# Sixteen more tokens gathered instead of computed densely, in a PEER block on one core

## The chip, the cores and the metric

The kernel runs on one core of a Trainium2 chip. The metric is the device time of one execution in microseconds (us). A profiled execution gives a trace of every engine: TensorE (PE, with its weight loads as PEld), VectorE (DVE), ScalarE (ACT), GpSimd (POOL) and SyncE (SP), which here only issues DMAs.

## What is computed

A residual block over 512 tokens of 1024 features. A token mixer (input projection, a recurrent branch and a convolution branch, output projection) comes first, and then the part that this study is about, a product-key expert layer. For each of 512 tokens and 8 heads it picks 16 of 16384 experts, so 128 experts for a token. An expert n has a row of u and a row of v, 1024 numbers each:

```python
def peer(xn, w_q, sub_keys, u_tab, v_tab):
    ...
    q = (t @ w_q).reshape(n_tok, PEER_HEADS, 2, PEER_HALF)
    sc = jnp.einsum("thpk,hpnk->thpn", q, sub_keys).astype(jnp.float32)
    s_top, i_top = lax.top_k(sc, PEER_TOPK)
    ...
    best, pos = lax.top_k(cand.reshape(n_tok, PEER_HEADS, kk), PEER_TOPK)
    ...
    g = jax.nn.softmax(best, axis=-1).astype(xn.dtype)
    ...
        ue = u_tab[ib]
        act = jax.nn.gelu(jnp.einsum("phkd,pd->phk", ue, tb))
        ve = v_tab[ib]
        return jnp.einsum("phk,phkd->pd", gb * act, ve)
```

Everything is float32. The layer's output is added to its input, and a last RMSNorm follows.

## The kernel before

The tokens are four tiles of 128. Tile 0 is the **gathered** tile: each of its tokens sits on one partition, and for each of its 128 expert choices an indirect DMA on POOL (L362) fetches 128 rows of u (tiles `ru`) or of v (`rv`), half a MB each. VectorE multiplies a `ru` with the tokens and sums along the row (L371); a `rv` is scaled and added into `acc0` (L385). That makes 256 gathers with 256 products of about 1.2 us. The order of the gathers is the list `gsched`; `gather_steps(n, left)` issues the next n of them and runs the waiting products until `left` remain open. The row buffers are three (`GR`) and, from the V stage on, five more (`DR`).

The other three tiles, 384 tokens (`TD`), are **dense**: for all 16384 experts the kernel computes gelu(u·x), multiplies it with a gate matrix that is zero except at the chosen experts, and multiplies the result with v. Experts come in 128 tiles of 128.

- An **h tile** is u·x for 128 experts and 384 tokens: 8 slices of the features, each as three matmuls (`mm3`, L147 to L149, tile `ph`), because a float32 number is split into a high and a low part (`hi_u` by ScalarE, L107; `lo_u` by VectorE or POOL, L108 or L745). `h_act` (L402) applies the gelu into `hg`. The first 56 (`SPILL`) are stored to memory and read back later (`hr`).
- The **top-k stage** (about 380 to 583 us) makes q and the scores on TensorE and the top-16s on VectorE, with an h tile in its steps.
- The **gate stage** (583 to 797 us) builds the gate matrix. It works in subs of 8 tokens (`OC`): VectorE makes two one-hot tensors (`oij` L714, `o12` L716, 2048 elements per partition), TensorE multiplies them, 16 matmuls for a sub (L726, L727, tile `pg`), and ScalarE evicts to the gate tile `stg` (L729). A step is two subs and one h tile (`h_step`). Eight steps fill `stg` for one token tile; there are 24 steps, in three blocks. After the first and the second block `stg`, 8 MB, is stored to memory in four DMAs on SP (L775), and 7 extra h tiles (`HB`) cover the store. In one step of three (`GSTEP`) a gather is issued.
- The **V stage** (797 us to the end) runs over the 128 expert tiles. For each it loads the rows of v, splits them (`hi_v` L107, `lo_v` L108), reads back the gates `gt` (of two token tiles; the third stayed in `stg`) and the stored gelus, multiplies them to `wf` (L847, L848), splits that into `wh` (ScalarE, L849) and `wl` (VectorE, L850), and adds to six PSUM accumulators `acc` with 18 matmuls of 512 columns (`v_mm`, L829, L830, L833). In the first 66 of these tiles an h tile is computed as well (`h_tile`). The gathers that are left are spread by weights: 2 for each of the first 66 tiles, `GTAIL` for the next 58, none for the last four. `GLEFT` products may stay open.

What sets the order: a scheduler is pinned off, so that each engine runs its instructions in the order of the program; queues are FIFO. A gather needs a free row buffer, which the product of an earlier gather releases, and its indices, which ScalarE copies (`eix`, L667).

## Time and profile before

| | |
|---|---|
| time, median of 3 runs | 1619.81 us |
| time, lowest and highest | 1617.53, 1622.06 us |
| time of the profiled execution | 1617.53 us |
| its span | 1615.4 us |
| PE busy | 1595.6 us, 99% |
| DVE busy | 1264.4 us, 78% |
| ACT busy | 688.2 us, 43% |
| POOL busy | 510.8 us, 32% |
| moved by DMA | 379.09 MB, mean 235 GB/s |

The span is what the engines' records cover; the time has a little before and behind it. Matmuls overlap, so a busy PE is not PE at its peak, and the shares are means over stages that have different limits: each stage has to be read by itself.

### The profile page before, as it was taken

What the parts mean: (1) busy time and instruction counts of PE and PEld (TensorE: products, weight loads), DVE (VectorE), ACT (ScalarE), POOL (GpSimd) and SP (SyncE); (2) the same over time, 40 slices, a digit from 0 to 9 for tenths busy, and PEclk for the clock granted to TensorE, in tenths of its full rate; (3) what the DMA queues carried; (4) which work ended last, traced back from release to release, by engine and by line L of the source; (5) the groups of instructions that cost most, each with busy time, mean ns of one, the idle gap of its engine ahead of it and who ended that gap; (6) DMA issues with size and microseconds to landing.
All of it is one profiled execution on the core that took longest, in us unless ns stands there. A gap on an engine that the chain in (4) does not pass through costs nothing.

```text
span 1615.4 us, 23573 instructions
## 1 busy us (share of the span) xinstructions
PE 1595.6 (99%) x8402; PEld 1412.5 (87%) x8402; DVE 1264.4 (78%) x2404; ACT 688.2 (43%) x1222; POOL 510.8 (32%) x379
## 2 busy tenths in 40 slices
PE   9999999999999999999999999999999999999997
PEld 8888888888988999999999888989998988887886
DVE  6666666645999997676878888888888789877767
ACT  7444444434333454454533433344333343333334
POOL 0000000004787840000045554545444554223231
PEclk9999999999999999999999999999999999999999
DMA  6222222334333356969499999999999999998884
GB/s 243 95 95 95 95 95 95 91 112 175 107 124 112 126 180 189 304 214 301 153 317 328 344 324 331 342 328 332 340 335 336 323 334 362 340 320 288 305 305 153
DMA packets 158453, 379.09 MB, mean 235 GB/s; under 512 B 14080, under 2 KB 78592, under 8 KB 158208
## 3 DMA queue, kind: packets, MB, share of 16 engines
q1 hardware_dynamic: 112832, 230.25, 41.6%
q0 software_dynamic: 36864, 134.23, 23.5%
q10 hardware_dynamic: 8640, 13.11, 2.3%
q8 instruction: 65, 1.06, 0.3%
q14 instruction: 52, 0.43, 0.1%
HBM read 345.56 MB, written 31.98 MB: 234 GB/s over the span
## 4 chain that ended last, share of the span: by engine, by line
PE 70%; DVE 9%; DMA 8%; issue 7%; POOL 3%; ACT 1%; SPq 1%; DVEq 0%; POOLq 0%; ACTq 0%
PE ph L147 7%; PE ph L149 7%; PE ph L148 7%; PE acc L830 7%; PE acc L833 6%; PE acc L829 6%; PE pin L149 6%; PE pin L147 6%; PE pin L148 6%; DMA ru<-in_u_tab_dram,eix 4%; DMA rv<-in_v_tab_dram,eix 3%; POOL rv L362 2%; PE pq L147 2%; PE pq L149 2%; PE pq L148 2%
## 5 line engine op out<-in xcount | busy, mean ns | idle before, releaser
L147 PE MATMUL ph<-a1h,hi_u 128*128 128x384 f32 x1024 | 346.3, 338 | 0.0
L149 PE MATMUL ph<-a1h,lo_u 128*128 128x384 f32 x1024 | 343.6, 336 | 0.6 <-POOL lo_u L108 0.4
L148 PE MATMUL ph<-a1l,hi_u 128*128 128x384 f32 x1024 | 342.7, 335 | 0.0
L830 PE MATMUL acc<-lo_v,wh 128*128 128x512 f32 x768 | 301.0, 392 | 5.1 <-DVE lo_v L108 5.1
L829 PE MATMUL acc<-hi_v,wh 128*128 128x512 f32 x768 | 299.5, 390 | 0.0
L362 POOL DMA_INDIRECT rv<-in_v_tab_dram,eix x128 | 168.1, 1313 | 265.0 <-ACT eix L667 229.7
L833 PE MATMUL acc<-hi_v,wl 128*128 128x512 f32 x768 | 238.7, 390 | 0.0
L362 POOL DMA_INDIRECT ru<-in_u_tab_dram,eix x120 | 161.0, 1341 | 216.7 <-ACT eix L667 178.3
L385 DVE SCALAR_TENSOR_TENSOR acc<-rv,w,acc 128x1024 f32<-128x1024 f32 x128 | 164.4, 1285 | 75.8 <-DMA rv<-in_v_tab_dram,eix 75.4
L107 ACT ACTIVATE hi_v<-raw_v 128x1024 fp32r<-128x1024 f32 x128 | 135.0, 1055 | 182.8 <-PE ph L148 169.3
L371 DVE SCALAR_TENSOR_TENSOR ru<-ru,t 128x1024 f32<-128x1024 f32 x128 | 155.7, 1222 | 57.0 <-DMA ru<-in_u_tab_dram,eix 56.9
L148 PEld LDWEIGHTS ph<-a1l,hi_u 128*128 128x128 f32 x1024 | 192.3, 188 | 2.6
L147 PEld LDWEIGHTS ph<-a1h,hi_u 128*128 128x128 f32 x1024 | 192.3, 188 | 2.6
L149 PEld LDWEIGHTS ph<-a1h,lo_u 128*128 128x128 f32 x1024 | 192.1, 188 | 1.5 <-POOL lo_u L108 0.8
L849 ACT ACTIVATE wh<-wf 128x384 fp32r<-128x384 f32 x128 | 67.0, 524 | 268.9 <-PE acc L830 193.0
L830 PEld LDWEIGHTS acc<-lo_v,wh 128*128 128x128 f32 x768 | 144.2, 188 | 38.9 <-DVE lo_v L108 10.1
L149 PE MATMUL pin<-a1h,lo_in 128*128 128x512 f32 x448 | 174.4, 389 | 0.3 <-POOL lo_in L108 0.3
L148 PE MATMUL pin<-a1l,hi_in 128*128 128x512 f32 x448 | 174.4, 389 | 0.0
L147 PE MATMUL pin<-a1h,hi_in 128*128 128x512 f32 x448 | 174.3, 389 | 0.0
L833 PEld LDWEIGHTS acc<-hi_v,wl 128*128 128x128 f32 x768 | 144.1, 188 | 30.7
L829 PEld LDWEIGHTS acc<-hi_v,wh 128*128 128x128 f32 x768 | 144.1, 188 | 27.4 <-ACT hi_v L107 0.2
L108 DVE TENSOR_TENSOR lo_v<-raw_v,hi_v 128x1024 fp32r<-128x1024 f32 x128 | 155.9, 1218 | 3.4 <-ACT hi_v L107 3.4
(199 smaller groups left out, 2469.9 us busy)
## 6 DMA issues: line engine op xcount, KB each, us to landing
raw_u<-in_uT_dram SPq DMA_DIRECT2D x128, 512.0 KB, 5.4
raw_v<-in_v_tab_dram SPq DMA_DIRECT2D x128, 512.0 KB, 5.6
raw_in<-in_w_in_dram SPq DMA_DIRECT2D x56, 512.0 KB, 3.3
gd<-stg SPq DMA_DIRECT2D x8, 2048.0 KB, 17.8
gt<-gd SPq DMA_DIRECT2D x128, 128.0 KB, 5.0
hd<-hg ACTq DMA_DIRECT2D x56, 192.0 KB, 3.4
hr<-hd SPq DMA_DIRECT2D x56, 192.0 KB, 5.5
raw_q<-in_w_q_dram SPq DMA_DIRECT2D x16, 512.0 KB, 3.2
```

Source lines behind the costliest of these rows:

```text
L107: act.activation(hi, raw, AF.Copy)
L108: lo_eng.tensor_tensor(lo, raw, hi, op=ALU.subtract)
L147: pe.matmul(pt, wh(k), xh(k), start=start and m == 0, stop=False)
L148: pe.matmul(pt, wh(k), xl(k), start=False, stop=False)
L149: pe.matmul(pt, wl(k), xh(k), start=False, stop=stop and m == n - 1)
L362: ins = pool.indirect_dma_start(out=rows, out_offset=None, in_=tab, in_offset=bass.IndirectOffsetOnAxis(ap=ix, axis=0))
L371: dq.append(lambda: dve.scalar_tensor_tensor(rows, rows, 1.0, t0, op0=ALU.mult, op1=ALU.mult, accum_out=d0[:, n:n + 1]))
L385: dq.append(lambda: dve.scalar_tensor_tensor(acc0, rows, w0[:, n:n + 1], acc0, op0=ALU.mult, op1=ALU.add))
L829: pe.matmul(accs[t][h], wh[:, ts], hi[:, hsl], start=first, stop=False)
L830: pe.matmul(accs[t][h], wh[:, ts], lo[:, hsl], start=False, stop=False)
L833: pe.matmul(accs[t][h], wl[:, ts], hi[:, hsl], start=False, stop=last)
L849: act.activation(wh, wf, AF.Copy)
```

## The change

The last 16 tokens (`TE`) leave the dense part and are gathered too. For them a gather holds 8 partitions to a token: partition 8e + k works on token e, and 16 gathers of u rows and 16 of v rows (`xxu`, `xxv`) cover their 128 experts each. So:

- h tiles, `hg`, `hr` and `hd` have 368 columns (`TDE`) and no longer 384. `wf` keeps 384 columns, the last 16 of them zeroed once in two fixed buffers; its second product has 112 columns.
- There are 46 subs and not 48: the last gate step has no one-hots and no gate matmuls.
- The normalised last token tile is made once more in rows (`tx`, two POOL operations), its 16 tokens go to memory and are read back with each token on 8 partitions (`te`, 16 DMAs on SP). Indices and gates of the 16 tokens go through memory in the same way (`eed`, `egd`, `ee`, `eg`).
- 32 gathers are added: first the 16 `xxu`, and behind the first head's `ru` the weights (`gather_xw`) and the 16 `xxv`, whose products go to `acce`. At V tile 48 (`XADD`) `acce` is split, and four matmuls of 512 columns sum each token's 8 partitions into the accumulators of the last token tile.
- `GSTEP` is now (1,): from the third gate step on a gather in every step, 22 in the stage and not 8.
- `DR` and `GLEFT` go from 5 to 4, `GTAIL` from 0.5 to 0.7.

```diff
+TE = 16
+TDE = TD - TE
...
-GSTEP = (1, 0, 0)
+GSTEP = (1,)
...
-DR = 5
-GTAIL = 0.5
+DR = 4
+GTAIL = 0.7
...
-GLEFT = 5
+GLEFT = 4
 GR = 3
+XADD = 48
...
+        tx = fp.tile([P, D], F32, tag="junk", name="tx", bufs=1)
+        pool.tensor_scalar(tx, xs[NTT - 1], r, None, op0=ALU.mult)
+        pool.tensor_tensor(tx, tx, n2b, op=ALU.mult)
...
+        act.dma_start(txd, tx[P - TE:, :])
...
+    def gather_xu(n):
+        rows = gather(u_tab, n, f"xxu{n}")
+        dq.append(lambda: dve.scalar_tensor_tensor(rows, rows, 1.0, te, op0=ALU.mult, op1=ALU.mult,
+                                                   accum_out=de[:, n:n + 1]))
...
+    def gather_xv(n):
+        rows = gather(v_tab, n, f"xxv{n}")
+
+        def add():
+            if n == 0:
+                acce.append(gp.tile([P, D], F32, tag="te", name="acce", bufs=1))
+                dve.tensor_scalar(acce[0], rows, de[:, 0:1], None, op0=ALU.mult)
+            else:
+                dve.scalar_tensor_tensor(acce[0], rows, de[:, n:n + 1], acce[0], op0=ALU.mult, op1=ALU.add)
...
-        mm3(pt[:, :TD], lambda k: hi[:, k * P:(k + 1) * P], lambda k: lo[:, k * P:(k + 1) * P],
-            lambda k: a1h[:, k, P:], lambda k: a1l[:, k, P:], range(KD))
+        mm3(pt[:, :TDE], lambda k: hi[:, k * P:(k + 1) * P], lambda k: lo[:, k * P:(k + 1) * P],
+            lambda k: a1h[:, k, P:P + TDE], lambda k: a1l[:, k, P:P + TDE], range(KD))
...
+            if s_ == 8:
+                for e in range(TE):
+                    sync.dma_start(te[e * EK:(e + 1) * EK, :], txd[e:e + 1, :].partition_broadcast(EK))
...
-    gsched = []
+    gsched = [(gather_xu, n) for n in range(TE)]
     for h in range(HEADS):
         for n in range(h * TOPK, (h + 1) * TOPK):
             gsched.append((gather_u, n))
+        if h == 0:
+            gsched.append((gather_xw, 0))
+            gsched.extend((gather_xv, n) for n in range(TE))
...
+        act.dma_start(eed, eall[last[1], last[0], :])
+        act.dma_start(egd, gall[last[1], last[0], :])
+        for e_, d_ in ((ee, eed), (eg, egd)):
+            pool.dma_start(e_, d_.rearrange("e (k n) -> (e k) n", n=TE))
...
-        NSUB = NDT * P // OC
+        NSUB = TDE // OC
...
-                gather_steps(GSTEP[(sub // 2) % len(GSTEP)], 2)
+                if sub // 2 == 1:
+                    act.activation(eei, ee, AF.Copy)
+                if sub // 2 > 1:
+                    gather_steps(GSTEP[(sub // 2) % len(GSTEP)], 2)
...
+    wfs = [dp.tile([P, TD], F32, name=f"wf{m}") for m in range(2)]
+    for wf in wfs:
+        dve.memset(wf[:, TDE:], 0.0)
...
-        dve.tensor_tensor(wf[:, TG:], stg[:, i, :], hv_[:, TG:], op=ALU.mult)
+        dve.tensor_tensor(wf[:, TG:TDE], stg[:, i, :P - TE], hv_[:, TG:], op=ALU.mult)
...
+        if i == XADD:
+
+            bf = dp.tile([P, TG], F32, tag="gt", name="bf", bufs=4)
+            br = strm.tile([P, TD], F32R, tag="wh", name="br", bufs=3)
+            dve.memset(bf[:, :P], 0.0)
+            dve.tensor_reduce(bf[:, P - TE:P], ident.rearrange("p (e k) -> p e k", k=EK), op=ALU.add, axis=AX.X)
+            act.activation(br[:, :P], bf[:, :P], AF.Copy, scale=GSC)
+            hi, lo = split(acce[0], "acce", dve)
+            for part in (hi, lo):
+                for h in range(2):
+                    pe.matmul(accs[NDT - 1][h], br[:, :P], part[:, h * 512:(h + 1) * 512], start=False, stop=False)
```

Line numbers move: the product of a u row, L371, becomes L388, with L394 for the new rows; that of a v row, L385, becomes L426; L714, L716 and L745 become L767, L769 and L798.

Where the order of the work changes, first VectorE in the second half of the gate stage's first block, two steps (`lo_u` belongs to the step's h tile). Before:

```order
L745 TENSOR_TENSOR lo_u102_5771<-raw_u102_5547,hi_u102_5721 128x1024
L714 TENSOR_TENSOR oij_14_5847<-io_5173,ij_5218 128x2048
L716 TENSOR_TENSOR o12_14_5848<-oij_14_5847,g12_5219 128x2048
L714 TENSOR_TENSOR oij_15_5851<-io_5173,ij_5218 128x2048
L716 TENSOR_TENSOR o12_15_5852<-oij_15_5851,g12_5219 128x2048
L745 TENSOR_TENSOR lo_u103_5855<-raw_u103_5549,hi_u103_5805 128x1024
L371 SCALAR_TENSOR_TENSOR ru0_5381,d0_2928<-ru0_5381,t0_2535 128x1024
```

The same place of the changed kernel:

```order
L798 TENSOR_TENSOR lo_u102_5807<-raw_u102_5580,hi_u102_5757 128x1024
L394 SCALAR_TENSOR_TENSOR xxu1_5664,de_2939<-xxu1_5664,te_2940 128x1024
L767 TENSOR_TENSOR oij_14_5886<-io_5201,ij_5246 128x2048
L769 TENSOR_TENSOR o12_14_5887<-oij_14_5886,g12_5247 128x2048
L767 TENSOR_TENSOR oij_15_5890<-io_5201,ij_5246 128x2048
L769 TENSOR_TENSOR o12_15_5891<-oij_15_5890,g12_5247 128x2048
L798 TENSOR_TENSOR lo_u103_5894<-raw_u103_5582,hi_u103_5844 128x1024
L394 SCALAR_TENSOR_TENSOR xxu2_5750,de_2939<-xxu2_5750,te_2940 128x1024
```

A product of 1024 elements now stands in each step, where one of the two steps had one.

Second, VectorE in the last third of the V stage, around tiles 101 to 105. Before:

```order
L847 TENSOR_TENSOR wf103_14473<-gt103_14471,hr103_14476 128x256
L848 TENSOR_TENSOR wf103_14473<-stg2_7120,hr103_14476 128x128
L385 SCALAR_TENSOR_TENSOR acc0_7785<-rv111_14427,w0_2927,acc0_7785 128x1024
L850 TENSOR_TENSOR wl102_14440<-wf102_14438,wh102_14439 128x384
L108 TENSOR_TENSOR lo_v102_14433<-raw_v102_14430,hi_v102_14432 128x1024
L847 TENSOR_TENSOR wf104_14515<-gt104_14513,hr104_14518 128x256
L848 TENSOR_TENSOR wf104_14515<-stg2_7120,hr104_14518 128x128
L850 TENSOR_TENSOR wl103_14475<-wf103_14473,wh103_14474 128x384
L847 TENSOR_TENSOR wf105_14555<-gt105_14553,hr105_14558 128x256
L848 TENSOR_TENSOR wf105_14555<-stg2_7120,hr105_14558 128x128
L108 TENSOR_TENSOR lo_v103_14468<-raw_v103_14465,hi_v103_14467 128x1024
L385 SCALAR_TENSOR_TENSOR acc0_7785<-rv112_14504,w0_2927,acc0_7785 128x1024
```

In the changed kernel:

```order
L426 SCALAR_TENSOR_TENSOR acc0_7812<-rv103_14386,w0_2934,acc0_7812 128x1024
L911 TENSOR_TENSOR wl101_14398<-wf1_7823,wh101_14397 128x384
L116 TENSOR_TENSOR lo_v101_14392<-raw_v101_14389,hi_v101_14391 128x1024
L908 TENSOR_TENSOR wf1_7823<-gt103_14473,hr103_14477 128x256
L909 TENSOR_TENSOR wf1_7823<-stg2_7177,hr103_14477 128x112
L426 SCALAR_TENSOR_TENSOR acc0_7812<-rv104_14425,w0_2934,acc0_7812 128x1024
L911 TENSOR_TENSOR wl102_14437<-wf0_7822,wh102_14436 128x384
L116 TENSOR_TENSOR lo_v102_14431<-raw_v102_14428,hi_v102_14430 128x1024
L908 TENSOR_TENSOR wf0_7822<-gt104_14512,hr104_14516 128x256
L909 TENSOR_TENSOR wf0_7822<-stg2_7177,hr104_14516 128x112
```

A tile before has a product in most cases and `wl`, `lo_v` and `wf` around it; now one stands in every tile, ahead of the tile's `wl` and `lo_v`. These rows say only what follows what on the engine.

## Rows read from the trace of the kernel before

**Rows 1.** The page's part 1: busy us (share) x instructions, by engine.
```profile
PE 1595.6 (99%) x8402; PEld 1412.5 (87%) x8402; DVE 1264.4 (78%) x2404; ACT 688.2 (43%) x1222; POOL 510.8 (32%) x379
```

**Rows 2.** Timeline of PE: start us, us, engine line operation, out<-in, shapes.
```profile
727.76 0.33 PE L149 MATMUL ph<-a1h,lo_u 128*128 128x384 f32 x1
...
735.91 0.33 PE L148 MATMUL ph<-a1l,hi_u 128*128 128x384 f32 x1
...
1419.64 0.39 PE L829 MATMUL acc<-hi_v,wh 128*128 128x512 f32 x1
...
1428.48 0.39 PE L830 MATMUL acc<-lo_v,wh 128*128 128x512 f32 x1
```

**Rows 3.** Waits, 380 to 590 us (total, times, longest); then the chain around 566.
```profile
DVE st L466 <- PE pc L515: 10.4, 4, 7.6
...
566.13 3.98 POOL lo_u L108
```

**Rows 4.** Timeline of DVE in the gate stage; idle time before and its releaser in brackets.
```profile
669.04 1.23 DVE L714 TENSOR_TENSOR oij<-io,ij 128x2048 f16<-128x2048 f16 x1 [1.20 <-PE pg L727]
...
676.12 1.22 DVE L714 TENSOR_TENSOR oij<-io,ij 128x2048 f16<-128x2048 f16 x1
...
682.05 1.22 DVE L714 TENSOR_TENSOR oij<-io,ij 128x2048 f16<-128x2048 f16 x1
```

**Rows 5.** Timeline of PE in the gate stage and at the first V matmul.
```profile
602.31 0.24 PE L726 MATMUL pg<-o,oij 128*128 128x128 f16 x1
...
608.39 0.24 PE L726 MATMUL pg<-o,oij 128*128 128x128 f16 x1
...
706.26 0.24 PE L726 MATMUL pg<-o,oij 128*128 128x128 f16 x1
...
708.09 0.42 PE L147 MATMUL ph<-a1h,hi_u 128*128 128x384 f32 x1
...
750.41 0.42 PE L147 MATMUL ph<-a1h,hi_u 128*128 128x384 f32 x1
...
797.17 0.39 PE L829 MATMUL acc<-hi_v,wh 128*128 128x512 f32 x1
```

**Rows 6.** Second store: SP and ACT timelines; stretch (PE, PEld, DVE, ACT, POOL, PEclk, DMA, GB/s).
```profile
710.38 0.38 SPq L775 DMA_DIRECT2D gd<-stg  x1
...
748.85 1.58 ACT L729 ACTIVATE stg<-pg 128x512 f32<-128x512 f32 x3 [6.70 <-DMA gd<-stg]
...
715.00:730.00 15.00, 15.00 (x88) 15.00 (x87) 4.99 (x6) 5.16 (x7) 1.68 (x1) 1.00 1.03 315
```

**Rows 7.** Waits of 800 to 1350 us: total us, times, longest.
```profile
DVE ru L371 <- DMA ru<-in_u_tab_dram,eix: 50.2, 41, 3.3
DVE acc L385 <- DMA rv<-in_v_tab_dram,eix: 31.0, 27, 3.3
...
PEld acc L830 <- DVE lo_v L108: 6.1, 7, 1.4
...
PE acc L830 <- DVE lo_v L108: 3.5, 6, 1.0
```

**Rows 8.** Two stretches of the V stage, columns as in the last line of rows 6.
```profile
800.00:1350.00 550.00, 546.32 (x2754) 494.93 (x2753) 459.78 (x637) 213.57 (x470) 262.61 (x201) 1.00 0.93 330
...
1400.00:1550.00 150.00, 148.82 (x654) 122.24 (x653) 114.32 (x179) 56.73 (x103) 38.83 (x27) 1.00 0.88 306
```

**Rows 9.** Timelines of POOL and DVE late in the V stage.
```profile
1475.18 3.62 POOL L362 DMA_INDIRECT rv<-in_v_tab_dram,eix  x1 [7.68 <-ACT eix L667]
...
1483.69 0.94 POOL L362 DMA_INDIRECT rv<-in_v_tab_dram,eix  x1 [3.09 <-ACT eix L667]
...
1484.76 1.29 DVE L385 SCALAR_TENSOR_TENSOR acc<-rv,w,acc 128x1024 f32<-128x1024 f32 x1 [4.97 <-DMA rv<-in_v_tab_dram,eix]
...
1488.10 1.28 DVE L385 SCALAR_TENSOR_TENSOR acc<-rv,w,acc 128x1024 f32<-128x1024 f32 x1
```

**Rows 10.** Tile view of rv: from the gather's issue to its landing.
```profile
DMA to landing us min/median/max: 4.2/7.0/9.8
```

More of the change, by code (lines that the diff above doesn't have):

```diff
@@ L83, in tile_block @@
     x2d = dram.tile([NTT, P, D], F32, name="x2d")
+    txd = dram.tile([TE, D], F32, name="txd")
+    eed = dram.tile([TE, P], F32, name="eed")
+    egd = dram.tile([TE, P], F32, name="egd")
+    EK = P // TE
     @contextmanager
@@ L349, in tile_block @@
     d0 = gp.tile([P, P], F32, name="d0")
+    ee = gp.tile([P, TE], F32, name="ee")
+    eg = gp.tile([P, TE], F32, name="eg")
+    eei = gp.tile([P, TE], I32, name="eei")
+    de = gp.tile([P, TE], F32, name="de")
+    te = gp.tile([P, D], F32, tag="te", name="te", bufs=1)
     ha = ctx.enter_context(tc.tile_pool(name="ha", bufs=1))
@@ L357, in gather @@
     def gather(tab, n, name):
-        ix = gidx.get(name, ei0[:, n:n + 1])
+        ix = gidx[name] if name in gidx else (eei if name[1] == "x" else ei0)[:, n:n + 1]
         rp, nb = rpool[gcnt[0] % len(rpool)]
@@ L372, in gather_u, with gather_xw @@
                                                    accum_out=d0[:, n:n + 1]))
+    def gather_xu(n):
+        rows = gather(u_tab, n, f"xxu{n}")
+        dq.append(lambda: dve.scalar_tensor_tensor(rows, rows, 1.0, te, op0=ALU.mult, op1=ALU.mult,
+                                                   accum_out=de[:, n:n + 1]))
+    def gather_xw(_):
+        act.activation(de, de, AF.Gelu_apprx_tanh)
+        dve.tensor_tensor(de, de, eg, op=ALU.mult)
+    acce = []
+    def gather_xv(n):
[6 more added lines that the diff above has]
+                dve.scalar_tensor_tensor(acce[0], rows, de[:, n:n + 1], acce[0], op0=ALU.mult, op1=ALU.add)
+        dq.append(add)
     def drain(left):
@@ L395, in h_mm @@
         pt = ps_a(f"ph{i}")
[L396 to L397 removed]
+        mm3(pt[:, :TDE], lambda k: hi[:, k * P:(k + 1) * P], lambda k: lo[:, k * P:(k + 1) * P],
+            lambda k: a1h[:, k, P:P + TDE], lambda k: a1l[:, k, P:P + TDE], range(KD))
         return pt
     def h_act(i, pt):
[L401 to L402 removed]
+        g = ha.tile([P, TDE], F32, tag="hg", name=f"hg{i}", bufs=AHEAD)
+        act.activation(g, pt[:, :TDE], AF.Gelu_apprx_tanh)
         if i >= NKEY - SPILL:
@@ L409, in h_get @@
         if i not in hg:
-            hg[i] = ha.tile([P, TD], F32, tag="hg", name=f"hr{i}", bufs=AHEAD)
+            hg[i] = ha.tile([P, TDE], F32, tag="hg", name=f"hr{i}", bufs=AHEAD)
             sync.dma_start(hg[i], hd[i - (NKEY - SPILL)])
         return hg[i]
-    hd = dram.tile([max(SPILL, 1), P, TD], F32, name="hd")
+    hd = dram.tile([max(SPILL, 1), P, TDE], F32, name="hd")
     hord = list(range(NKEY - SPILL, NKEY)) + list(range(NKEY - SPILL))
@@ L659, in gather_release @@
             f, a = gsched[p]
-            if f is not gather_w:
-                names.append(("ru" if f is gather_u else "rv") + str(a))
+            if f not in (gather_w, gather_xw):
+                names.append({gather_u: "ru", gather_v: "rv", gather_xu: "xxu", gather_xv: "xxv"}[f] + str(a))
             p += 1
@@ L665, in gather_release @@
             for m, nm in enumerate(names):
-                c = int(nm[2:])
-                tc.keep_in_program_order(act.activation(t[:, m:m + 1], eall[:, 0, c:c + 1], AF.Copy))
+                c = int(nm.lstrip("rxuv"))
+                e = ee[:, c:c + 1] if nm[0] == "x" else eall[:, 0, c:c + 1]
+                tc.keep_in_program_order(act.activation(t[:, m:m + 1], e, AF.Copy))
                 gidx[nm] = t[:, m:m + 1]
@@ L675, in gather_steps @@
             gpos[0] += 1
-            if f is not gather_w:
+            if f not in (gather_w, gather_xw):
                 n -= 1
@@ L704, in tile_block @@
         dve.scalar_tensor_tensor(g12[:, :, 1, :], by_sub(ptg), GSC, g12[:, :, 0, :], op0=ALU.mult, op1=ALU.subtract)
+        last = (NTT - 1, slice(P - TE, P))
+        act.dma_start(eed, eall[last[1], last[0], :])
+        act.dma_start(egd, gall[last[1], last[0], :])
+        for e_, d_ in ((ee, eed), (eg, egd)):
+            pool.dma_start(e_, d_.rearrange("e (k n) -> (e k) n", n=TE))
         iob = io.unsqueeze(1).to_broadcast([P, OC, P, 2])
@@ L759, in mid @@
                     for u in (sub, sub + 1):
[L760 removed]
+                        if u < NSUB:
+                            gate_mm(u, *ohs.pop(u))
                     for u in (sub + OB, sub + OB + 1):
@@ L790, in tile_block @@
     accs = [[ps_b(f"acc{t}_{h}") for h in range(2)] for t in range(NDT)]
-    gdone = sum(1 for f, _ in gsched[:gpos[0]] if f is not gather_w)
-    ng = 2 * P - gdone
+    gdone = sum(1 for f, _ in gsched[:gpos[0]] if f not in (gather_w, gather_xw))
+    ng = 2 * (P + TE) - gdone
     wts = [2 if i < NKEY - nlag else GTAIL if i < NKEY - 4 else 0 for i in range(NKEY)]
@@ L842, in tile_block @@
         sync.dma_start(gt, gd[i])
-        wf = dp.tile([P, TD], F32, tag="wf", name=f"wf{i}", bufs=2)
+        wf = wfs[i % 2]
         wh = strm.tile([P, TD], F32R, tag="wh", name=f"wh{i}", bufs=3)
```

3 lines of the change are left out of this document (removed).

## The prediction

> **What bounds the kernel now.** I began with busy time by engine. TensorE (PE) is busy for 99% of the span and VectorE (DVE) for 78% [rows 1], so the first question for each part is whether PE really works there or waits in hidden places. The matmul timeline gives the price of a column [rows 2]: from 727.76 to 735.91 us there are 47 pitches of 384-column matmuls, 8.15 / 47 = 173.4 ns each; from 1419.64 to 1428.48 there are 39 pitches of 512 columns, 226.7 ns each. The slope is (226.7 - 173.4) / 128 = 0.417 ns per column. The waits then show where PE is not the limit. Up to 583 us, in the top-k stage, DVE waits on PE only four times, 10.4 us in all, and the chain at the stage's end runs through POOL's split, 566.13 to 570.11, before PE goes on [rows 3]. In the gate stage DVE and PE are nearly level [rows 4, 5], and each of the two 8 MB stores of the gate tile holds up the next block [rows 6]. In the V stage PE is the limit, but close behind it are the gathers: DVE waits 81.2 us on 68 late landings [rows 7], while the DMA engines are at a share of 0.93 [rows 8].
>
> **The shorter h tiles in the V stage, -10.6 us.** Sixteen columns at 0.417 ns are 6.67 ns; times 24 matmuls of an h tile and 66 tiles: 10.56 us. The gain lies on PE, so it counts whole if nothing else fills it. Bounds: 0 (pitch unchanged) and -10.6.
>
> [...]
>
> **The 23 h tiles before the gate stage, -0.2 us.** They lose 23 x 24 x 6.67 ns = 3.7 us of PE, but DVE's top-k chain and POOL's split (566.13 to 570.11) decide when PE goes on [rows 3]. Bounds 0 and -3.7; I take nearly nothing, because DVE hardly ever waits for PE there. The two POOL operations that build tx, the sixteen broadcasts and the four small index and gate transfers go into that stage or just behind it. The broadcasts are sixteen issues on SP's queue, 0.38 us each by the store's issue [rows 6], 6 us in all, in front of weight loads that are issued three steps ahead; they and the transfers are used first in the gate stage. I cost them at nothing; a POOL operation that delayed the top-k chain would cost its own time, at most the 3.98 us of POOL's split [rows 3]. The zeroing of two strips of 16 columns and the shorter second product into wf go at nothing too, beside DVE's idle time in the V stage.
>
> **The gate stage, +4.7 us.** A PE step goes from 602.31 to 608.39, 6.08 us [rows 5]; 24 x 6.67 ns less makes 5.92. A DVE step takes 676.12 to 682.05 = 5.93 us without a product and 669.04 to 676.12 = 7.08 with one [rows 4]. Before, one, three and two steps of the three blocks hold a product; now four, eight and all that are left. So with a product DVE sets the step, 1.16 us over PE's 5.92. What that does, block by block:
> - Block 1: the products come in its second half, and one-hots are made a step ahead. The last gate matmul ends 0.5 us later by my stepping through the order.
> - Its store: from 710.38 to 748.85, 38.5 us, is the second store [rows 6]; the first is alike. The DMA engines are full then (1.03 [rows 6]), so one more gather of 0.52 MB at 315 GB/s costs 1.65 us. The eight h tiles that cover it are also 1.3 us shorter. Block 2 therefore begins 2.1 us later.
> - Block 2: eight products instead of three, against a lead that DVE earns while the store is awaited. From its first to its last gate are six steps that now take 6.7 us each instead of 6.3: 4.6 us late at its end (before, its last gate ran from 706.26 to 708.09 [rows 5]). The second store adds 1.5: 6.1 late.
> - Block 3: before, from 750.41, where the block's second gate ends, to the first V matmul at 797.17 [rows 5] there are six steps and three h tiles. Now there are five steps of 6.65 (33.25) and three tiles of 4.03 (12.1), and the 1.83 us of gate matmuls of the last step are gone: 756.5 + 33.25 + 12.1 = 801.85, 4.7 later than 797.17.
>
> Bounds: -1 (the products fit into DVE's lead everywhere, the h tiles are shorter and the last step's 1.83 us are gone, the stores still late) and +9 (no lead at all: 7.08 us in the six steps of block 2 and the five of block 3, 6 x 0.38 + 5 x 0.43 = 4.4 more). I take the stepped value.
>
> **Joining the sixteen tokens, +2 us.** At tile 48 there are four more 512-column matmuls, 4 x 0.2267 = 0.9 us. Besides them DVE and ScalarE make a split, some copies and a small reduction in a tile whose margin is narrow. The nearest rows are the split and the wait on it: DVE lo_v delays PE by 1.0 us at most in one go, and weight loads by 1.4 [rows 7]. Bounds 0.9 and 4; I take the matmuls and one such wait.
>
> **The waits of the first 66 V tiles, +3.5 us.** The gathers per tile stay the same (3.08), but PE's tile gets 0.16 us shorter, so a landing that was just in time is late. DVE's 81.2 us of waiting reached PE as only 3.5 us on matmuls and 6.1 on weight loads [rows 7]: two tiles of cushion lie between. That cushion shrinks by 2 x 0.16 = 0.32 us a tile. Bounds: 0 and the whole gain given back, 10.6 (the DMA engines set the pace). I count it in one tile of six: 66 x 0.32 / 6 = 3.5, since about one of seven DVE waits reached PE.
>
> **The last 58 tiles, +4 us.** Of 256 gathers 8 were done in the gate stage and 248 left; now it is 288 less 22, or 266. The pace gives 66 tiles a weight of 2 and 58 tiles one of 0.7, no longer 0.5: 266 x 40.6 / 172.6 = 62.6 gathers there, where it was 248 x 29 / 161 = 44.7, so 1.08 a tile and not 0.77, and every tile has a product. DVE itself has room: from product to product 1484.76 to 1488.10 = 3.34 us [rows 9], against a PE tile of 18 x 0.2267 = 4.08. The gathers have less. Four row buffers instead of five and four products left open mean that a buffer goes round in three tiles, 12.24 us: landing, then about 4.4 us for issue, product and the DVE work queued in between. So PE loses nothing up to a landing of 12.24 - 4.4 = 7.8 us; the median of the v rows' gathers, the only ones late in the stage, is now 7.0 and the longest 9.8 [rows 10]. Eighteen more gathers of 0.524 MB in 240 us add 38 GB/s to 306, and the share of 0.88 [rows 8] becomes about 0.99. Bounds: 0, and 13 at a mean landing of 8.5: (8.5 + 4.4) / 3 - 4.08 = 0.22 us x 58. I take 4, near the lower end, as the median is still on the right side.
>
> **The sum.** -10.6 - 0.2 + 4.7 + 2.0 + 3.5 + 4.0 = +3.4 us on the profiled execution (span 1615.4, time 1617.53). The three runs have a median of 1619.81, 2.3 higher; the same difference there gives **1623 us**. About 0.3%, 4.9 us, is what a measurement of this kernel can tell from no change: 1615.0 to 1624.7 count as the same, and the forecast lies just inside.
>
> **The rivals.**
> - *The gain arrives whole.* The V stage keeps its 10.6 us, its waits do not grow, and DVE's lead swallows the products of the gate stage: -10.6 - 0.2 + 0 + 2.0 = -8.8, 1611 us. For it: DVE's 81 us of waiting hardly reach PE now [rows 7], and DVE is busy only 460 of 550 us there [rows 8]. Against it: the stores already decide when blocks 2 and 3 start [rows 6], and they share full DMA engines with more gathers. Chance 0.21.
> - *Gathers that land late set the pace of the last 58 tiles* (slower). The mechanism is the round of four buffers; it decides from a landing of 7.8 us. At 8.5 the tail costs 13, and the first half 6 instead of 3.5: +14.9, 1634.7 us. For it: the DMA share near 0.99, and that the POOL gather instruction takes 3.62 us at 1475.18 but 0.94 at 1483.69 [rows 9], so issue stretches too. Against it: the median lands in time today. Chance 0.20.
>
> [...]
> - *The gate stage loses its upper bound*, +9 rather than +4.7, the rest as forecast: +7.7, 1627.5 us. For it: every added product sits on a DVE that is already level with PE [rows 4, 5]. Against it: DVE earns a lead in each store. Chance 0.13.
> - *A matmul of 368 columns is no faster than one of 384*, because its weight load sets the pitch: the -10.6 is gone, +14, 1633.8 us. For it: a weight load takes 1412.5 us / 8402 = 168 ns on the mean [rows 1], nearly the pitch of 173. Against it: the pitch at 512 columns follows the columns at 0.417 ns [rows 2]. Chance 0.06.
>
> That the columns are not removed at all is excluded: in the order of the changed kernel the gelu of every h tile reads 368 of them.
>
> **How the numbers follow.** The forecast has 0.40, the rivals 0.21, 0.20, 0.13 and 0.06. The range runs from 1612, where the first rival lies up to a microsecond, to 1636, the second rival with its bound. Faster by over 0.3%: the first rival and a sliver of the forecast, 0.22. Slower: the second and fourth rival, 0.26, most of the third, 0.08, and the upper end of the forecast, 0.04, so 0.38. Within 0.3%: the rest, 0.40. The likeliest case on its own runs from 1617 to 1628.
>
> **What would show it.** Right, if the h matmuls stand 166.7 ns apart, the first V matmul comes at about 801.9, the gate steps with a product last 7.08 us, eviction after a store comes 2 and then 6 us later, and the DMA share of the tail is near 0.99 with landings of 7 to 8 us. The tail is the weakest term: landings beyond 8 us and PE waiting on lo_v in every third tile would mean the second rival; a tail at 4.08 us a tile and a DVE without new waits the first. If the first V matmul came at 797 or earlier, the gate term is wrong; if the pitch stays at 173 ns, the first term is.

## The result and the profile after

The changed kernel takes 1634.94 us (median of 12 runs, 1624.22 to 1641.7), the kernel before 1620.12 (median of 12, 1617.53 to 1624.9). The ratio is 1.0086, with a 95% interval of 1.0069 to 1.0103: **slower, by about 14.8 us**. That lies inside the range that was given, at its upper end; the forecast of no change, 1623 us, was 12 us too low. The change's runs also spread over 17.5 us and those of before over 7.4.

The profiled execution of the change took 1629.56 us, one of its quicker ones, with a span of 1627.8, 12.4 more than before. Part 1 of its page, to be read beside [rows 1]:

```profile
span 1627.8 us, 23699 instructions
...
PE 1582.1 (97%) x8374; PEld 1393.5 (86%) x8374; DVE 1293.1 (79%) x2454; ACT 687.4 (42%) x1240; POOL 588.1 (36%) x415
```

PE is busy 13.5 us less and the span is 12.4 us longer, so PE waits for something 26 us longer. Where, is read from PE's timeline at the edges of the stages. Before (the first V matmul is in [rows 5]), the starts of tiles 66 and 124, and the last matmul:

```profile
1351.26 0.39 PE L829 MATMUL acc<-hi_v,wh 128*128 128x512 f32 x1
...
1590.41 0.39 PE L829 MATMUL acc<-hi_v,wh 128*128 128x512 f32 x1
...
1607.35 0.39 PE L833 MATMUL acc<-hi_v,wl 128*128 128x512 f32 x1
```

The same places after, with the first V matmul ahead of them:

```profile
800.78 0.50 PE L886 MATMUL acc<-hi_v,wh 128*128 128x512 f32 x1 [1.59 <-ACT wh L910]
...
1349.19 0.39 PE L886 MATMUL acc<-hi_v,wh 128*128 128x512 f32 x1
...
1593.75 0.39 PE L886 MATMUL acc<-hi_v,wh 128*128 128x512 f32 x1
...
1619.08 0.39 PE L890 MATMUL acc<-hi_v,wl 128*128 128x512 f32 x1
```

| stretch | before | after | difference | in the prediction's sum |
|---|---|---|---|---|
| start to the first V matmul | 797.17 | 800.78 | +3.6 | +4.5 |
| first 66 V tiles | 554.09 | 548.41 | -5.7 | -5.1 (-10.6, +2.0, +3.5) |
| next 58 tiles, "the tail" | 239.15 | 244.56 | +5.4 | +4.0 |
| last four tiles to the last matmul's end | 17.3 | 25.7 | +8.4 | no term |
| behind the last matmul | 7.7 | 8.3 | +0.6 | no term |

Three stretches came out within 1.4 us of their terms. The last four tiles, which had none, cost the most.

**The tail.** Waits from 1350 us to the end (engine, line, what it waited for: total us, times, longest):

```profile
POOL rv L379 <- ACT eix L715: 73.0, 30, 5.7
...
DVE acc L426 <- DMA rv<-in_v_tab_dram,eix: 29.1, 13, 3.8
DVE ru L388 <- DMA ru<-in_u_tab_dram,eix: 12.9, 9, 2.7
PE acc L887 <- DVE lo_v L116: 7.8, 8, 1.8
```

VectorE waits 42 us for landings, and PE's waits are on `lo_v`, which stands behind the waiting product. That VectorE waits does not by itself cost PE time, for before it waited longer in the same stretch:

```profile
DVE acc L385 <- DMA rv<-in_v_tab_dram,eix: 44.4, 17, 5.0
...
DVE ru L371 <- DMA ru<-in_u_tab_dram,eix: 6.7, 7, 2.1
```

There the 58 tiles took only 2.5 us more than their matmuls (58 tiles of 18 pitches of 0.2267 us are 236.6). But VectorE was busy for 114.3 of 150 us then [rows 8] and is for 122.5 now, so less room is left to catch up. POOL waits for the indices that ScalarE copies. A row buffer that is not free would show as POOL waiting for a product; in the view of the `rv` tiles that is one wait of 0.3 us. The stretch that answers to the second of [rows 8] and the landing that answers to [rows 10]:

```profile
1400.00:1550.00 150.00, 147.29 (x645) 120.33 (x643) 122.50 (x198) 55.69 (x110) 57.80 (x39) 1.00 0.96 342
```
```profile
DMA to landing us min/median/max: 4.9/7.6/10.0
```

The DMA share rose from 0.88 to 0.96 and the median landing from 7.0 to 7.6. POOL's share rose most: 39 instructions take 57.8 us, 1.48 each, where 27 took 38.8, 1.44 each.

**One stall, followed through.** POOL late in the tail, then VectorE:

```profile
1569.19 3.14 POOL L379 DMA_INDIRECT rv<-in_v_tab_dram,eix  x1 [2.31 <-ACT eix L715]
1572.64 3.02 POOL L379 DMA_INDIRECT rv<-in_v_tab_dram,eix  x1 [0.30 <-issue]
1576.47 0.94 POOL L379 DMA_INDIRECT rv<-in_v_tab_dram,eix  x1 [0.81 <-ACT eix L715]
1583.07 3.14 POOL L379 DMA_INDIRECT rv<-in_v_tab_dram,eix  x1 [5.65 <-ACT eix L715]
```
```profile
1574.56 0.28 DVE L909 TENSOR_TENSOR wf<-stg,hr 128x112 f32<-128x112 f32 x1
1578.66 1.28 DVE L426 SCALAR_TENSOR_TENSOR acc<-rv,w,acc 128x1024 f32<-128x1024 f32 x1 [3.82 <-DMA rv<-in_v_tab_dram,eix]
1579.86 0.55 DVE L911 TENSOR_TENSOR wl<-wf,wh 128x384 fp32r<-128x384 f32 x1
1580.33 1.22 DVE L116 TENSOR_TENSOR lo_v<-raw_v,hi_v 128x1024 fp32r<-128x1024 f32 x1
...
1581.80 0.27 DVE L909 TENSOR_TENSOR wf<-stg,hr 128x112 f32<-128x112 f32 x1
1581.99 1.28 DVE L426 SCALAR_TENSOR_TENSOR acc<-rv,w,acc 128x1024 f32<-128x1024 f32 x1
...
1585.31 1.28 DVE L426 SCALAR_TENSOR_TENSOR acc<-rv,w,acc 128x1024 f32<-128x1024 f32 x1
...
1592.04 1.28 DVE L426 SCALAR_TENSOR_TENSOR acc<-rv,w,acc 128x1024 f32<-128x1024 f32 x1 [3.33 <-DMA rv<-in_v_tab_dram,eix]
...
1593.71 1.22 DVE L116 TENSOR_TENSOR lo_v<-raw_v,hi_v 128x1024 fp32r<-128x1024 f32 x1
```

The product at 1578.66 belongs to the gather that POOL began at 1569.19: it landed 9.4 us after. The last gather was begun at 1583.07 and its product ran at 1592.04, when PE was about to begin tile 124; before, the last product ran at 1582.08 and PE reached tile 124 at 1590.41. So VectorE has its last product behind it some 10 us later than it did, and PE reaches tile 124 only 3.3 us later. PE's waits from there on (before, one of 0.5 us on `lo_v`):

```profile
PE acc L887 <- DVE lo_v L116: 2.6, 2, 1.8
PE acc L886 <- ACT hi_v L115: 1.4, 2, 1.3
PE acc L886 <- ACT wh L910: 0.7, 1, 0.7
```

Its weight loads wait 7.2 us there, and 1.3 before; the two lists overlap in part.

The rows also show one turn of a round. Behind the product at 1578.66 comes `wf` (1581.80); from it ScalarE makes `wh` and then copies the index, POOL begins the gather at 1583.07, and its product, the third one on, runs at 1592.04. That is 13.4 us, where three tiles take PE 12.24.

Why is a landing awaited at all, when `GLEFT` leaves four products open? Because the V stage lies behind the part in which the order is pinned: that the scheduler is off, as the section on the kernel before has it, holds only up to the end of the gate stage. In the V stage the scheduler places the products itself: in VectorE's order of the changed kernel the product of the gather that belongs to tile 101 (`rv104`) stands ahead of `wl102`, one tile on, and so through the whole tail. It stood so before, too (`rv111`, tile 101), but with 0.77 gathers a tile.

**Theory A**: in the tail gather, landing and product form a round of three tiles through VectorE's order (`wf`, `wh`, index, gather, landing, product), and at one product a tile it is too tight. **Theory B**: the DMA engines are full. **Theory C**: the row buffers set the round, as the prediction said. **Theory D**, added later: what counts is how long the gather instruction on POOL takes.

### The profile page after: what moved, and what is told of

The parts are those of the page before. It is cut to its first block, busy times and chain, and to the rows that moved or that the text cites. A ratio compares the mean times of both kernels' runs of the same rounds, so it can differ in the third digit from the quotient of the medians.

```text
span 1627.8 us, 23699 instructions
## 1 busy us (share of the span) xinstructions
PE 1582.1 (97%) x8374; PEld 1393.5 (86%) x8374; DVE 1293.1 (79%) x2454; ACT 687.4 (42%) x1240; POOL 588.1 (36%) x415
## 5 line engine op out<-in xcount | busy, mean ns | idle before, releaser
L157 PE MATMUL ph<-a1h,lo_u 128*128 128x368 f32 x1024 | 338.4, 330 | 3.3 <-POOL lo_u L116 2.6
L155 PE MATMUL ph<-a1h,hi_u 128*128 128x368 f32 x1024 | 340.6, 333 | 0.0
L156 PE MATMUL ph<-a1l,hi_u 128*128 128x368 f32 x1024 | 337.4, 330 | 0.0
L379 POOL DMA_INDIRECT rv<-in_v_tab_dram,eix x128 | 186.0, 1453 | 201.6 <-ACT eix L715 172.0
L890 PE MATMUL acc<-hi_v,wl 128*128 128x512 f32 x768 | 239.9, 392 | 0.0
L379 POOL DMA_INDIRECT ru<-in_u_tab_dram,eix x122 | 168.2, 1379 | 191.7 <-ACT eix L715 164.0
L426 DVE SCALAR_TENSOR_TENSOR acc<-rv,w,acc 128x1024 f32<-128x1024 f32 x128 | 164.6, 1286 | 57.2 <-DMA rv<-in_v_tab_dram,eix 56.9
L388 DVE SCALAR_TENSOR_TENSOR ru<-ru,t 128x1024 f32<-128x1024 f32 x128 | 155.6, 1223 | 58.4 <-DMA ru<-in_u_tab_dram,eix 54.6
```

The costliest lines, as they stand in the source:

```text
L155: pe.matmul(pt, wh(k), xh(k), start=start and m == 0, stop=False)
L156: pe.matmul(pt, wh(k), xl(k), start=False, stop=False)
L157: pe.matmul(pt, wl(k), xh(k), start=False, stop=stop and m == n - 1)
L379: ins = pool.indirect_dma_start(out=rows, out_offset=None, in_=tab, in_offset=bass.IndirectOffsetOnAxis(ap=ix, axis=0))
L388: dq.append(lambda: dve.scalar_tensor_tensor(rows, rows, 1.0, t0, op0=ALU.mult, op1=ALU.mult, accum_out=d0[:, n:n + 1]))
L426: dq.append(lambda: dve.scalar_tensor_tensor(acc0, rows, w0[:, n:n + 1], acc0, op0=ALU.mult, op1=ALU.add))
```

## The experiments

Each ran beside the kernel before on the same chip; medians and ratios to it. Stage times are from each run's own profiled execution.

| run | median us | ratio, 95% interval | first V matmul | 66 tiles | tail | last four |
|---|---|---|---|---|---|---|
| the change | 1634.94 | 1.0086 (1.0069 to 1.0103) | 800.8 | 548.4 | 244.6 | 25.7 |
| 1 last gather earlier | 1627.99 | 1.0046 (1.0027 to 1.0064) | 801.6 | 548.2 | 256.1 | 16.8 |
| 2 late products | 1618.76 | 0.9994 (0.9983 to 1.0005) | 801.8 | 547.8 | 238.0 | 17.0 |
| 3 both | 1617.62 | 0.9985 (0.9974 to 0.9996) | 800.1 | 548.6 | 239.9 | 16.7 |
| 4 GTAIL 0.5 | 1623.70 | 1.0019 (1.0002 to 1.0037) | 800.7 | 553.0 | 243.0 | 17.0 |
| 5 one tile, tied | 1643.41 | 1.0142 (1.0121 to 1.0164) | 799.3 | 551.0 | 258.7 | 25.1 |
| 6 before, with both edits | 1614.53 | 0.9971 (0.9959 to 0.9983) | 797.3 | 552.3 | 238.1 | 16.8 |
| 7 columns only | 1604.85 | 0.9902 (0.9882 to 0.9922) | 789.3 | 544.7 | 239.0 | 17.2 |
| 8 late everywhere | 1615.00 | 0.9972 (0.9958 to 0.9986) | 800.2 | 549.3 | 238.7 | 16.7 |
| 9 as 8, gather in every 2nd step | 1607.27 | 0.9927 (0.9902 to 0.9953) | 791.3 | 549.3 | 237.5 | 16.7 |
| 10 as 8, lo_u on POOL | 1630.10 | 1.0061 (1.0042 to 1.0081) | 814.6 | 549.0 | 238.4 | 16.7 |
| 11 as 8, gather in every 3rd step | 1607.29 | 0.9924 (0.9906 to 0.9943) | 788.6 | 553.6 | 237.2 | 16.7 |
| 12 only every 2nd step | 1630.04 | 1.0072 (1.0053 to 1.0090) | 792.6 | 553.2 | 248.5 | 25.0 |

A stage time is that of one execution. The change and runs 1 to 5 and 8 have the same program up to the first V matmul, and there it comes at 799.3 to 801.8; differences of that size say nothing.

**1, the last gather four tiles earlier.**

```diff
-    wts = [2 if i < NKEY - nlag else GTAIL if i < NKEY - 4 else 0 for i in range(NKEY)]
+    wts = [2 if i < NKEY - nlag else GTAIL if i < NKEY - 8 else 0 for i in range(NKEY)]
```

> The last gather goes out with tile 119 and not with tile 123; nothing else is changed. Theory A (in the tail a product stands one tile behind its gather in VectorE's order, so gather issue, landing and product form a round of three tiles; the last four tiles begin while VectorE is still behind): the time from the start of tile 124 to the last accumulator matmul falls from 25.7 us to 18 to 20, the 58 tiles of the tail stay at about 244 us, and the kernel gains 5 to 7 us on the change (about 1629). Theory B (the DMA engines are full in the tail, so the same bytes in fewer tiles cost what the end gains): 1635 or more, the end shorter and the tail longer by as much.

The end fell from 25.7 to 16.8 us and the median by 7, as theory A had it. But in the profiled execution (1632.73, the second slowest of its eight) the tail grew by 11.5, which looks like theory B. Alone this does not decide; the next run does.

**2, the products tied to their place.**

```diff
-        dq.append(lambda: dve.scalar_tensor_tensor(acc0, rows, w0[:, n:n + 1], acc0, op0=ALU.mult, op1=ALU.add))
+        def add():
+            ins = dve.scalar_tensor_tensor(acc0, rows, w0[:, n:n + 1], acc0, op0=ALU.mult, op1=ALU.add)
+            if gpos[0] >= 230:
+                tc.keep_in_program_order(ins)
+
+        dq.append(add)
...
```

The products of the u rows have the same edit. `gpos` counts along `gsched`; 230 is about where the tail begins.

> In the tail each product is tied to its place in the program, four gathers behind its own, so that it stands four tiles behind its gather on VectorE and not one. Same bytes, same instructions. Theory A: VectorE's waits on landings in the tail, 42 us in the profiled run of the change, fall under 10 us, and the 58 tiles take 237 to 240 us, not 244.6; the end stays as it is or grows by 2 us, since four products then come together there: 1629 to 1633. Theory B (DMA engines full): the tail stays at 244 or more. Theory C (the step of the prediction as it was worded: the row buffers set the round): a later product frees its buffer later, so the tail gets longer, by 5 us or more.

No instruction and no byte is different. VectorE's order in the tail is, and with it a few places of ScalarE's order and the order of TensorE's last matmuls. The 16 us are gone: tail 238.0 (against 236.6 for the matmuls alone), end 17.0. From the start of a gather in the tail to its product it is now 15.1 us at the median, and 8.6 in the change. The stretch in this run:

```profile
1400.00:1550.00 150.00, 150.00 (x663) 124.22 (x662) 129.21 (x206) 58.48 (x115) 47.63 (x40) 1.00 0.98 354
```

PE never pauses while the DMA engines are at 0.98 and move 354 GB/s, more than the 342 at which the change stalled. Theory B falls. Theory C falls as well: buffers are freed later here, and nothing gets longer. Theory A's size was underestimated: the end returned too, which it did not expect of this edit alone. VectorE is no longer behind when the last tiles begin. Its list of waits from 1350 us has 1.0 us on `rv` and 4.5 on `ru` landings in the place of 42.

**3, both edits**, with the last products drained one in each of tiles 120 to 123.

> Both edits together, and the last four products spread over tiles 120 to 123. Theory A: tail 237 to 240 us and end 18 to 19: 1620 to 1624, level with the kernel before. Theory B: no better than the better one of the two alone. Theory C: slower than the change.

1617.62 us, better than expected, and level with run 2 within the spread. The gathers lie in the same tiles as in run 1, whose tail took 256.1 us; here it takes 239.9, so it was not the DMA engines there either.

**4, GTAIL back to 0.5.**

```diff
-GTAIL = 0.7
+GTAIL = 0.5
```

> GTAIL back to 0.5: 48 gathers in the tail and not 62.6 (0.83 a tile, as before the change 0.77), 3.30 in each of the first 66 tiles and not 3.08. Theory A: tail and end return most of 5.4 + 8.4 us, the first 66 tiles lose 2 to 5 as the waits there grow: 1626 to 1631. Theory B: the first part, at a DMA share of 0.94, loses what the tail gains: 1634 to 1638.

The first 66 tiles lost 4.6 us, the end returned 8.7, the tail only 1.6 of its 5.4, and the median fell by 11 to 1623.70, somewhat more than expected. Theory B's 1634 to 1638 is missed: the first part pays for the gathers that move there, but less than half of what the end and the tail return.

**5, one tile behind, but tied.** Theory D has to be told apart: run 2 also moved the product from ahead of `wl` to behind it, and there the gather instruction mostly takes 1.05 us.

```diff
 (run 2, and)
-        gather_steps(pace[i], GLEFT)
+        gather_steps(pace[i], GLEFT if i < NKEY - nlag else 1)
```

> As the run with late products, but only one product stays open in the tail: each is again one tile behind its gather, as in the change, yet it stands between wl and lo_v, where the late products stood, and not ahead of wl. Theory A (the distance sets the round): slow like the change, tail 243 to 250 us and VectorE waiting over 30 us on landings there, 1630 to 1638. Theory D (what counted in the run with late products was the place beside wl, at which the gather instruction on POOL came through in 1.05 us and not in up to 3.14): about as fast as late products, tail 238 to 240, 1618 to 1622.

1643.41 us, slower than the change itself, with a tail of 258.7 and an end of 25.1. Waits of this run from 1350 us:

```profile
POOL rv L379 <- ACT eix L726: 92.3, 30, 10.0
ACT wh L921 <- DVE wf L920: 80.4, 24, 9.8
...
DVE acc L433 <- DMA rv<-in_v_tab_dram,eix: 40.8, 22, 5.1
```

The round is to be seen here as a ring: POOL waits for the index behind `wh`, `wh` waits for `wf` on VectorE, VectorE waits in a product for the landing. The buffers and the instructions are those of run 2 and the time is 25 us longer, so the place of the products in VectorE's order decides, which is theory A.

The run does not set theory D apart, as it was meant to. The gather instructions of its tail take 1.64 us on the mean, as in the change (1.63), and not as in run 2 (1.27). And their length is a part of the round. In the tail of the change the 14 gathers whose instruction took 2.5 us or more landed 9.0 us after it began, on the mean, and the 31 that took at most 1.2 us landed after 7.1; nine of the 14 were awaited, for 23.8 of the 38.4 us that VectorE waited for these 65. Four tiles of distance have room for either, one tile mostly for the short ones only. How much of the 25 us is distance and how much the longer instruction, no run shows.

**6, the kernel before with both edits.**

> The kernel before the change, with the two edits of the best version so far (products tied four and more gathers behind in the tail, last gather with tile 119). It tells what these edits are worth without the change. If the round of three tiles hardly bound before (2.2 us of stalls in its tail, 0.6 at the end), it gains 1 to 3 us: 1617 to 1619, and the change with the same edits is then level with it. If it gains nothing (1620), the whole difference to the best version is the change's own; if it gains over 5, the change is a loss with or without the edits.

It gains 5 us (1614.53), more than expected. Its profiled execution has 1.1 us of that in the tail, 0.6 at the end and 1.8 in the first 66 tiles, which the edits touch only by the pace. So the round cost something before the change as well, and a kernel that gains from the edits is the right one to compare with: 0.9971 here and 0.9985 and 0.9972 in runs 3 and 8. With the tail mended, the change is worth nothing as it stands.

**7, the columns alone.**

```diff
-    gsched = [(gather_xu, n) for n in range(TE)]
+    gsched = []
...
-XADD = 48
+XADD = -1
-GSTEP = (1,)
+GSTEP = (1, 0, 0)
-DR = 4
+DR = 5
-GLEFT = 4
+GLEFT = 5
...
```

GTAIL is 0.5 there, and the copies of `te` go too.

> The gain alone: 368 columns and 46 subs, but none of the 32 added gathers and no joining, with GSTEP, DR, GTAIL and GLEFT as before the change; the last sixteen tokens get no expert output. By the prediction's terms: -10.6 in the first 66 V tiles less at most 3.5 of waits, and the first V matmul 2 to 4 us earlier than 797.2: 1604 to 1610. If the waits of the first part take the columns' gain back, since the DMA engines set the pace there: 1613 to 1617.

1604.85 us, inside the expectation. The first 66 tiles are 9.4 us shorter than before, so the column term of 10.6 arrives nearly whole and costs 1.2 of waits. The gate stage was mispriced in its parts: the first V matmul comes at 789.27, 7.9 earlier than before, and what this run leaves out then costs 800.78 - 789.27 = 11.5 us. Run 11 below tells that it is the gathers in the stage: up to that matmul it has everything that the change adds, but 7 gathers in the stage and not 22, and the V stage begins as early. The first V matmul in run 7, then in run 11:

```profile
789.27 0.39 PE L879 MATMUL acc<-hi_v,wh 128*128 128x512 f32 x1
```
```profile
788.57 0.39 PE L897 MATMUL acc<-hi_v,wh 128*128 128x512 f32 x1
```

The prediction had only the sum right.

**8, late products in the whole V stage.**

> The best version so far, with the products tied to their place through the whole V stage and not in the tail only. In the first 66 tiles VectorE waits some 75 us on landings, and about 11 us of that reach TensorE. If these too come from where the order puts the products, the first part gets 3 to 6 us shorter: 1612 to 1615. If they come from the row buffers and from DMA engines that are full (share 0.94), it stays at 1617 to 1619, or gets slower where a product ties up VectorE that the scheduler had placed well.

In VectorE's order only some five places differ from run 3, so this is close to a repeat of it. The median meets the first expectation, but not in the way that it names: the first part did not move (549.3 and 548.6), and the 2.6 us between the medians are what two sets of runs differ by.

**9, a gather in every second gate step.**

```diff
-GSTEP = (1,)
+GSTEP = (1, 0)
```

> The run with late products everywhere, and in the gate stage a gather in every second step, so 11 in the stage and not 22; the V stage has 277 and not 266. The gate stage's gathers cost 11.5 us there by the difference between the change and the run with columns only (first V matmul 800.8 against 789.3). If that cost is linear in the 14 added gathers, 11 fewer bring 6 to 8 us there; if the V stage is at its DMA limit (share 0.93 and 0.98), 11 gathers of 0.524 MB at 345 GB/s cost up to 16.7 us, if it is not, some 2 to 4. First V matmul 793 to 796; total 1610 to 1613 if the V stage has room, 1618 to 1625 if it has not.

1607.27 us, better than either expectation and **faster than both kernels**: 0.9927 to the kernel before. The first V matmul comes at 791.3, 8.9 earlier than in run 8, and the first 66 tiles with more gathers take no longer. The V stage had room; the gate stage had none.

**10, the split on POOL.**

```diff
-                dve.tensor_tensor(lo, raw, hi, op=ALU.subtract)
+                lo_eng.tensor_tensor(lo, raw, hi, op=ALU.subtract)
```

with `lo_eng` POOL in every second step from the fifth on.

> The run with late products everywhere, and in every second gate step from the fifth on the low part of the split (lo_u) is made by POOL and not by VectorE, which frees 1.2 us of VectorE in such a step and costs POOL 2.5. If VectorE's products are what makes the gate stage longer, the first V matmul comes 3 to 6 us earlier than 800: 1610 to 1613. If the stores or the queue of gathers on POOL decide, it stays at 800 or later: 1615 to 1620, as lo_u then stands behind a gather that waits for its buffer.

A miss: the first V matmul comes at 814.6, 14 us later. POOL in this run's gate stage:

```profile
688.63 5.69 POOL L809 TENSOR_TENSOR lo_u<-raw_u,hi_u 128x1024 fp32r<-128x1024 f32 x2 [4.98 <-PE pg L791]
694.47 1.76 POOL L379 DMA_INDIRECT xxu<-in_u_tab_dram,eei  x1
699.21 1.69 POOL L379 DMA_INDIRECT xxu<-in_u_tab_dram,eei  x1 [2.98 <-DVE xxu L399]
```

A split takes 2.85 us there and the gather stands behind it, so both the h tile and the product come later. It does not refute that VectorE's products lengthen the stage, since POOL brought delays of its own.

**11, a gather in every third step.**

> As the last version with a gather in every second gate step, now in every third, as before the change: 7 gathers in the stage and 281 in the V stage. If each gather in the gate stage still costs some 0.8 us there (9 us for 11), 4 fewer bring 2 to 3, and the first V matmul comes at 788 to 790; if the V stage still has room (it took 11 more at no cost, at shares of 0.95 and 0.99), 1603 to 1606. If it is full, 4 gathers cost 1.5 us each there, and it is level or slower: 1607 to 1611.

Level with run 9 (1607.29): the first V matmul comes 2.8 us earlier, the first 66 tiles take 4.3 more. This is where the V stage's room ends. The fair comparison for runs 9 and 11 is run 6, the kernel before with the same edits in the tail: 0.9927 and 0.9924 against 0.9971, each to the kernel before on its own chip. So the change itself is worth about 0.45%, some 7 us, once both costs are mended.

**12, run 9's edit alone.**

> The change with GSTEP (1, 0) alone: products one tile behind in the tail and the last gather with tile 123, as in the change. If the two costs are separate, the gate stage gives 9 us back (first V matmul at 791 to 793) and the tail and the end keep theirs, or cost 1 to 4 more with 65 gathers there instead of 62.6: 1626 to 1631, so 5 to 9 better than the change. If the round of the tail takes up what the gate stage gives: 1633 to 1637.

1630.04, 5 us better than the change: the gate stage gives 8.2 back, the tail and the first part take 8.8 more in its profiled execution, and the end keeps its 25. So the gate stage's cost can be mended by itself, but with the products one tile behind, part of what it gives is lost again in the V stage, which in run 9 took none of it. Both have to be mended.

## Why the prediction was right and wrong

**The columns: right.** The h matmuls of the change, timeline of PE:

```profile
726.75 0.33 PE L156 MATMUL ph<-a1l,hi_u 128*128 128x368 f32 x1
...
735.25 0.33 PE L156 MATMUL ph<-a1l,hi_u 128*128 128x368 f32 x1
```

These are 51 pitches in 8.50 us, 166.7 ns as forecast; the rival of a pitch that does not follow the columns is out. Run 7 shows the gain in the V stage, 9.4 of 10.6 us.

**Before the gate stage: right, within the scatter.** The term was -0.2; the first gate matmul moved from 583.08 to 583.35. In the other runs with 368 columns it comes at 580.87 to 582.70, 0.8 earlier than before at the median, so a little of the 3.7 us does arrive.

**The gate stage: right in the sum, wrong in the parts.** +3.6 against +4.5 together with the term before. A VectorE step with a product takes 7.07 us (691.52 to 698.59), as read from [rows 4]:

```profile
691.52 1.23 DVE L767 TENSOR_TENSOR oij<-io,ij 128x2048 f16<-128x2048 f16 x1
...
698.59 1.22 DVE L767 TENSOR_TENSOR oij<-io,ij 128x2048 f16<-128x2048 f16 x1
```

The evictions behind the stores:

```profile
669.46 2.07 ACT L782 ACTIVATE stg<-pg 128x512 f32<-128x512 f32 x4 [7.25 <-DMA raw_u<-in_uT_dram]
...
751.93 2.07 ACT L782 ACTIVATE stg<-pg 128x512 f32<-128x512 f32 x4 [7.67 <-DMA gd<-stg]
```

Before they began at 668.60 and, as [rows 6] has it, at 748.85; they come 0.9 and 3.1 us later, not 2 and 6. What failed is the reading that each store by itself holds up the next block. From the first gate matmul of a block's last step to the next block's first it took 35.20 us before, at both stores; in run 7 33.91 and 33.94, so the 1.3 us of the eight shorter tiles came as a gain, and so it did in runs 9, 11 and 12; in the change, with 22 gathers in the stage, it took 35.05 and 34.66. Run 7 shows 7.9 us of gain in all up to the first V matmul, from the columns and the missing sub, and 11.5 us of cost; the sum hid both, and that it came out is luck. Of the 11.5 us, 4.4 lie between block 3's first gate matmul and the first V matmul, 2.7 in block 2 from its first step to its last, and 1.9 from block to block. The 2.3 us ahead of the first gate matmul (581.04 in run 7, 583.35 in the change) can be scatter, since runs with the change's program up to there come as early as 580.87.

**The joining, +2: too low.** In the change's execution tiles 48 and 49 take 9.03 and 9.82 us where their neighbours take 8.11, so 2.6 more. In the ten runs that join the tokens as well, the two tiles take 2.9 to 8.4 more, 3.8 at the median, with waits for landings among it.

**The first 66 tiles' waits, +3.5: too high.** Run 7 has 1.2; the change has 548.41 - 544.70 = 3.7 over it, of which the joining is 2.6, so 2.3 of waits in all.

**The last 58 tiles, +4: right in size in this execution, wrong in the cause.** The three-tile round and its limit of 7.8 us of landing were the right arithmetic (the 4.4 us for the rest of the round, for which the prediction gives no row, lie between 1578.66 and 1583.07 in the turn above), and the median landing came to 7.6, just under it. But the sentence that four row buffers and four open products set the round was wrong. The kernel has seven buffers there, three (`GR`) and four (`DR`), and takes the two kinds in turn, so that a buffer comes round after six or eight gathers; and runs 2 and 5 have the same buffers and differ by 25 us. It is VectorE's order in the tail, where the scheduler put a product one tile behind its gather. The excerpt of the order that stands ahead of the prediction shows it (`rv104` ahead of `wl102`), and was read only for the number of products. A fifth row buffer together with the change was not tried.

**The end, no term: the step that failed.** The sum ended with tile 123. A round without slack leaves VectorE late, and behind the last gather there are only four tiles to catch up: 8.4 us here. Both costs also vary with each landing, which would explain why the median of the runs lies 5.4 above the profiled one, with before 2.6; that is argued, not shown.

**The rivals.** The second was priced at 1634.7 and the median is 1634.94, but that is luck. It names the gathers that land late, which is right, and the round of four buffers, which is not, and it had 13 us in the tail and none at the end. The first, the gain that arrives whole, was priced at 1611. Runs 7, 9 and 11 come below that, 7 without the added gathers and 9 and 11 with the tail mended as well, which is worth 5 us to the kernel before by itself. The range held by its upper end, which the second rival had set; the forecast itself, no change, did not.

## What to carry over

When work is added to a loop whose loads are awaited, read from the order how far behind its load each consumer stands, per engine, and compare issue, landing and the rest of the round with that distance; open-work counts in the source do not say it where a scheduler places the instructions. A stage that balances two engines to a few per cent was the wrong place here for extra work on one of them (steps of 6.08 us on PE before, and of 5.93 or, with a product, 7.08 on VectorE, [rows 4, 5]): 11 gathers moved from the gate to the V stage brought the first V matmul 9 us forward, at no cost behind it. And a sum by stage needs a term for the last tiles, since lateness that a long loop hides is paid at its end, here with 8.4 us.

## What the runs showed of the hardware

The time that a gather's instruction took on POOL went in part with what VectorE did at that moment. With VectorE idle it took 0.94 us (1576.47 above, inside the wait of 1574.84 to 1578.66). Eighteen of the 65 in the tail began up to 0.31 us before a product ended ahead of `wl`, `lo_v`, `wf`, `wf` without a gap (once with a `wf` ahead of `lo_v`). Twelve of them took 3.02 or 3.14 us, which is until 0.82 us behind the end of that chain, and the other six 0.95 to 1.13. Of all 65, 48 met a VectorE that was busy for over 95% of the first 1.5 us; these took 1.83 us on the mean, and the ten that found it idle for over half of that took 1.03. In run 2, where the gathers come as `wl` ends and a product begins, most take the same short time:

```profile
1482.32 1.05 POOL L379 DMA_INDIRECT rv<-in_v_tab_dram,eix  x1 [3.16 <-ACT eix L726]
1486.37 1.05 POOL L379 DMA_INDIRECT rv<-in_v_tab_dram,eix  x1 [3.01 <-ACT eix L726]
```

Beside the product that ran there it took 1.05 us, 0.11 more than with VectorE idle. What decides whether a gather takes 1 us or 3 beside the chain of `wl`, `lo_v` and `wf`, no run shows. The gathers with the longer instruction landed later, 9.0 against 7.1 us after its begin (under run 5), but how much of the change's loss that makes is open.

That queues are FIFO, as the section on the kernel before has it, shows in its trace: on POOL's, ScalarE's and SP's queue the 256, 60 and 556 DMAs landed in the order in which they were issued.

Nearly full DMA engines were not a limit by themselves: at a share of 0.98 and 354 GB/s (run 2, 1400 to 1550 us) PE never paused, where 15.1 us lay between a gather's start and its product, at the median.
